# Seven block products in place of eight in the feed-forward networks, and one table function for the gate

## The chip, the cores and the metric

The kernel runs on one core of a Trainium2 chip. The metric is the time of one execution on the device in microseconds (us); the time before is the median of three runs, 1405.89 us (1405.14 to 1406.78). Engines: TensorE (PE) multiplies matrices, VectorE (DVE) and ScalarE (ACT) work element by element, GpSimd (POOL) does a few powers, and SyncE (SP) issues the weight loads. Matrix products end in PSUM, of which the kernel has six banks of 128 x 512 for products and two for transposes; all other tiles are in SBUF.

## The reference

256 rows of 1024 numbers go through two stacks. The first has one layer (attention, a chunked recurrent mixer, gates) and one feed-forward network. The second has two layers, each a feed-forward network, an attention stage with a memory, and a second feed-forward network. All five networks are of the same form, with 1024 inputs and 2816 hidden columns:

```python
def swiglu(h, w_gate, w_up, w_down):
    return (jax.nn.silu(h @ w_gate) * (h @ w_up)) @ w_down
...
        h = rmsnorm(x, ffn1_norm[i])
        x = x + 0.5 * swiglu(h, ffn1_w_gate[i], ffn1_w_up[i], ffn1_w_down[i])
```

All of it is float32. The networks take most of the span; the change is in them.

## The kernel before

**Splitting.** A float32 number is used as the sum of a rounded part (hi, type fp32r, tiles wh) and a rest (lo, tiles wl). `split` (L203) makes them: ACT casts (L204), DVE subtracts (L205). A product of two such numbers is three matmuls (`mm3`, L225): hi x hi, hi x lo, lo x hi. One matmul has 128 rows of output (a row tile t; there are two), 128 of contraction and 512 columns.

**The stream of weights.** The weights lie in DRAM as pieces of 128 x 2048 in the order of use. SP loads them into tiles `raw` (L199), three at a time and at most two pieces ahead. Each piece is split in two halves of 128 x 1024, each in two steps of 512 (`SPLIT_W`). A half is asked for by the matmuls (`half`, L220), and then halves up to four further are split (`SPLIT_AHEAD`). The results are in eight buffers (`W_BUFS`); a buffer is free when the matmuls on it have ended.

**A network** (`ffn_body`, L335) goes through its 2816 hidden columns in eleven blocks of 256 (j = 0 to 10). Gate-up (`gu`, L346): for each row tile a sum over 8 contraction steps into one PSUM bank, 256 gate columns beside 256 up columns, 24 matmuls on four halves. ACT takes the tanh of half the gate (th, L355), DVE makes silu from it (L356) and multiplies by the up part (hid, L358). `turn` (L369) transposes the hid of both row tiles on PE (4 transposes), and splits them into hh and hl (L381). Down (`dn`, L386): 12 matmuls for each row tile on two halves, summed over all blocks in two banks for each row tile; these four banks are taken for the whole network, so two are left for the gate-up products. The order is gu(0, j), dn(0, j-1), gu(1, j), dn(1, j-1) (L409): 72 matmuls and 4 transposes for a block.

**Order.** PE's order is written by hand; the class `Order` counts matmuls and puts transposes in where their data are due. On ACT, DVE and SP a scheduler sets the order when the program is built; what is marked `crit()` goes first. Once built, each engine works through its list in that order, and an instruction that waits holds all those behind it.

**Around the networks.** `boundary` (L309) transposes the new rows and makes the left operands uh and ul from uf (L299). The output projections of the attention stages go row tile by row tile (L1192), each over two column halves. `during` (L416) starts the preparation of the memory in the middle of a network.

## Time and profile before

| | |
|---|---|
| median of the runs | 1405.89 us |
| profiled execution | 1406.4 us, of which the span 1404.6 us |
| PE busy | 1385.3 us, 99% |
| DVE busy | 922.8 us, 66% |
| ACT busy | 763.6 us, 54% |
| one block of a network | 17.05 us |

The span goes from the first to the last instruction. A busy share is a mean over the span. A matmul's duration in the profile is longer than the distance to the next one, since matmuls overlap; the same is true, by less, of DVE and ACT. So what a row of many costs is read from start to start.

### The profile page before, as it was taken

The page shows a single profiled execution, that of the slowest core. Times are in us where ns is not written, and L with a number is a line of the kernel's source. Part 1 is how long each engine was busy: PE and PEld are TensorE (multiplying, and loading weights), DVE is VectorE, ACT ScalarE, POOL GpSimd, SP SyncE. Part 2 cuts the span into 40 slices and gives each one's busy share as a digit, 9 for nine tenths or more (in the row PEclk, how much of TensorE's full clock was granted, in tenths as well). Part 3 has the DMA queues.
Part 4 walks back from the last instruction along what each step waited for, and adds up shares of the span by engine and source line. Part 5 has one row for each costly group of instructions (what it writes and reads, how often), then busy time and mean ns, then how long its engine had stood idle before and what let it go on. Part 6 is the DMA issues. An engine that isn't in the chain of part 4 may idle for free.

```text
span 1404.6 us, 18011 instructions
## 1 busy us (share of the span) xinstructions
PE 1385.3 (99%) x6598; PEld 1126.6 (80%) x6598; DVE 922.8 (66%) x1789; ACT 763.6 (54%) x1527; POOL 58.2 (4%) x59
## 2 busy tenths in 40 slices
PE   8999999999999999999999999999999989999998
PEld 6777888888888888877888888888888767888887
DVE  7866587555585575768576665765756787755554
ACT  6556555444474454668565444644545568544442
POOL 0000000000010000022000000000000121000000
PEclk9999999999999999999999999999999999999999
DMA  8534546555446455454255555555454532455540
GB/s 291 174 122 158 180 142 237 192 191 189 180 157 233 180 180 180 168 197 161 91 183 191 195 187 194 207 191 197 164 206 155 182 120 94 172 188 194 192 180 30
DMA packets 37081, 246.59 MB, mean 176 GB/s; under 512 B 4736, under 2 KB 5760, under 8 KB 8064
## 3 DMA queue, kind: packets, MB, share of 16 engines
q1 hardware_dynamic: 35568, 243.09, 48.2%
q10 hardware_dynamic: 1424, 2.34, 0.5%
q8 instruction: 52, 0.85, 0.2%
q14 instruction: 37, 0.30, 0.1%
HBM read 244.37 MB, written 1.05 MB: 175 GB/s over the span
## 4 chain that ended last, share of the span: by engine, by line
PE 90%; DVE 6%; POOL 2%; ACT 1%; issue 1%; DMA 0%; SPq 0%; DVEq 0%; POOLq 0%; ACTq 0%
PE bank L149 86%; PE trbank L154 4%; POOL fac L261 2%; DVE wl L205 2%; DVE ms L953 1%; ACT p L454 1%; DVE nm L452 1%; DVE z L957 1%; DMA h<-in_x_dram 0%; DVE p L464 0%; DVE p L450 0%; DVE z L1015 0%; DVE p L1052 0%; DVE z L1017 0%; DVE z L1018 0%
## 5 line engine op out<-in xcount | busy, mean ns | idle before, releaser
L205 DVE TENSOR_TENSOR wl<-raw,wh 128x512 fp32r<-128x512 f32 x908 | 580.5, 686 | 194.4 <-ACT wh L204 187.6
L204 ACT CAST wh<-raw 128x512 fp32r<-128x512 f32 x908 | 513.0, 619 | 238.2 <-PE bank L149 227.9
L149 PE MATMUL bank<-wh,uh 128*128 128x512 f32 x1248 | 501.3, 402 | 0.0
L149 PE MATMUL bank<-wl,uh 128*128 128x512 f32 x1248 | 489.5, 392 | 0.0
L149 PE MATMUL bank<-wh,ul 128*128 128x512 f32 x1248 | 489.3, 392 | 0.0
L149 PEld LDWEIGHTS bank<-wh,ul 128*128 128x128 f32 x1248 | 234.6, 188 | 52.6
L149 PEld LDWEIGHTS bank<-wh,uh 128*128 128x128 f32 x1248 | 234.9, 188 | 48.8 <-issue 1.9
L149 PEld LDWEIGHTS bank<-wl,uh 128*128 128x128 f32 x1248 | 235.2, 188 | 46.1 <-DVE wl L205 0.3
L149 PE MATMUL bank<-wh,hh 128*128 128x512 f32 x440 | 172.8, 393 | 0.0
L149 PE MATMUL bank<-wl,hh 128*128 128x512 f32 x440 | 172.0, 391 | 0.0
L149 PE MATMUL bank<-wh,hl 128*128 128x512 f32 x440 | 172.0, 391 | 0.0
L355 ACT ACTIVATE th<-bank,rs 128x256 f32<-128x256 f32 x110 | 52.3, 475 | 179.2 <-PE bank L149 178.4
L356 DVE SCALAR_TENSOR_TENSOR th<-th,bank 128x256 f32<-128x256 f32 x110 | 46.3, 421 | 153.2 <-ACT th L355 153.2
L149 PEld LDWEIGHTS bank<-wl,hh 128*128 128x128 f32 x440 | 82.7, 188 | 18.0
L149 PEld LDWEIGHTS bank<-wh,hl 128*128 128x128 f32 x440 | 82.6, 188 | 17.9
L149 PEld LDWEIGHTS bank<-wh,hh 128*128 128x128 f32 x440 | 82.7, 188 | 17.6
L204 ACT CAST hh<-trbank 128x512 fp32r<-128x512 f32 (+1 forms) x60 | 33.1, 551 | 55.8 <-PE trbank L154 55.8
L261 POOL TENSOR_TENSOR r<-ms,mhalf 128x1 f32<-128x1 f32 x22 | 18.4, 838 | 909.5 <-DVE ms L271 909.5
L358 DVE SCALAR_TENSOR_TENSOR hid<-bank,rs,th 128x256 f32<-128x256 f32 x110 | 53.2, 484 | 3.6
L205 DVE TENSOR_TENSOR hl<-trbank,hh 128x512 fp32r<-128x512 f32 (+1 forms) x60 | 38.8, 646 | 16.5 <-ACT hh L204 13.5
L261 POOL TENSOR_TENSOR fac<-ms,mhalf 128x4 f32<-128x4 f32 (+2 forms) x26 | 38.4, 1477 | 246.8 <-DVE ms L954 139.3
L154 PEld LDWEIGHTS trbank<-cst,hid 128*128 128x128 f32 x220 | 27.6, 140 | 8.1
(223 smaller groups left out, 940.1 us busy)
## 6 DMA issues: line engine op xcount, KB each, us to landing
raw<-in_weights_dram SPq DMA_DIRECT2D x226, 1024.0 KB, 4.9
mem<-in_mem_dram ACTq DMA_DIRECT2D x4, 512.0 KB, 5.5
Tb<-in_rel_dram SPq DMA_DIRECT2D x3, 512.0 KB, 5.8
h<-in_x_dram SPq DMA_DIRECT2D x4, 256.0 KB, 3.8
raw<-in_weights_dram SPq DMA_DIRECT2D x2, 512.0 KB, 7.4
gf<-in_rows_dram SPq DMA_DIRECT2D x1, 512.0 KB, 4.1
out_dram<-h SPq DMA_DIRECT2D x2, 256.0 KB, 2.0
out_dram<-h SPq DMA_DIRECT2D x4, 128.0 KB, 1.8
```

The lines of the kernel that those rows point to most:

```text
L149: pe.matmul(out=out, lhsT=lhsT, rhs=rhs, start=start, stop=stop)
L154: pe.transpose(out=out, in_=in_, identity=ident if identity is None else identity)
L204: act.copy(out=hi, in_=src)
L205: dve.tensor_tensor(out=lo, in0=src, in1=hi.bitcast(F32), op=ALU.subtract)
L261: pool.tensor_tensor(out=dst, in0=src, in1=mhalf[:, 0:n], op=ALU.pow)
L355: act.activation(out=th, in_=acc[:, 0:256], func=AF.Tanh, scale=rh[t])
L356: dve.scalar_tensor_tensor(out=th, in0=th, scalar=1.0, in1=acc[:, 0:256], op0=ALU.add, op1=ALU.mult)
L358: dve.scalar_tensor_tensor(out=hd, in0=acc[:, 256:512], scalar=r2[t], in1=th, op0=ALU.mult, op1=ALU.mult)
L452: dve.tensor_reduce(out=nm, in_=s, axis=AX.X, op=ALU.max, negate=True)
L454: act.activation(out=p[:, j, a, 0:n], in_=s[:, j], func=AF.Exp, bias=nm[:, j:j + 1], accum_out=sums[:, j, a:a + 1])
L953: dve.tensor_reduce(out=ms, in_=sq, axis=AX.X, op=ALU.add)
L957: dve.tensor_tensor(out=v, in0=v, in1=fac.unsqueeze(2).to_broadcast([128, n, w]), op=ALU.mult)
```

## The change

The last six of the eleven blocks of each network are taken in three groups of two (`GROUPS`). For such a pair the gate-up product is a product of a 2 x 2 matrix of blocks (two row tiles by two halves of the contraction) with another (two halves of the contraction by two column blocks). It is computed as seven block products for eight, P1 to P7, each of 12 matmuls on two halves into one PSUM bank. Their right operands are sums of loaded pieces b11, b12, b21, b22, made by DVE in place (`add`: 8 of 128 x 1024 for a group) and then split like the others; three of the pieces are split as loaded. The left operands are four differences and sums of uf, made and split once in a network (`group_operands`, after block 0). The results are combined by DVE in tiles `jo` (`joined`, seven of 128 x 512 for a group; one more copy on ACT).

The order within a group on PE is P1, dn(1, a), dn(0, a), P6, P2, P5, dn(0, b), P7, dn(1, b), P3, P4, where a and b are two earlier blocks. Blocks 0 to 4 are computed as before, in the order gu(0, j), gu(1, j), dn(0, j-1), dn(1, j-1). The halves are now a list of jobs; the casts on ACT are held in the order of that list (`in_order`). A half is split in one step of 1024, and there are six operand buffers for eight. The pieces b12 and b22 get tiles of their own (`rawx`).

The gate is one ACT function, silu, with the row scale; the second DVE operation is gone. The output projections go column half by column half. The memory preparation starts after block 4 and has one tile for two.

```diff
 RAW_BUFS = 3
-W_BUFS = 8
+W_BUFS = 6
 C_BUFS = 11
 C2_BUFS = 10
 SPLIT_AHEAD = 4
 LOAD_AHEAD = 2
 CRIT = 300
-SPLIT_W = 512
+SPLIT_W = 1024
+
+GROUPS = 3
...
+    piece_at = {}
+
+    def add_job(key, piece, work):
+
+        at_job[key] = len(jobs)
+        jobs.append((key, piece, work))
+
+    def plain(i):
+        for m in range(2):
+            add_job((i, m), i, lambda i=i, m=m: raws[i][:, 1024 * m:1024 * m + 1024])
...
-            r = wp.tile([128, 2048], F32, tag="raw", bufs=RAW_BUFS, name="raw")
+            if i in kept:
+                r = kept[i][0].tile([128, 2048], F32, tag="tx", bufs=2, name="rawx")
+            else:
+                r = wp.tile([128, 2048], F32, tag="raw", bufs=RAW_BUFS, name="raw")
...
     def split(hi, lo, src):
-        act.copy(out=hi, in_=src)
+        c = act.copy(out=hi, in_=src)
         dve.tensor_tensor(out=lo, in0=src, in1=hi.bitcast(F32), op=ALU.subtract)
+        return c
+
+    order = [None]
+
+    def in_order(inst):
+
+        if order[0] is not None:
+            tc.add_manual_dep(inst.ins, order[0].ins.name,
+                              mybir.DependencyInfo(mybir.DependencyClass.NoSync, mybir.DependencyReason.DATA),
+                              reason="order of the operands")
+        order[0] = inst
...
+        while stream["split"] < min(n, len(jobs)):
+            key, piece, work = jobs[stream["split"]]
+            load_to(piece + 1 + LOAD_AHEAD)
+            r = work()
             hi = wp.tile([128, 1024], FR, tag="wh", bufs=W_BUFS, name="wh")
             lo = wp.tile([128, 1024], FR, tag="wl", bufs=W_BUFS, name="wl")
             for s in range(0, 1024, SPLIT_W):
-                split(hi[:, s:s + SPLIT_W], lo[:, s:s + SPLIT_W], r[:, 1024 * m + s:1024 * m + s + SPLIT_W])
-            parts[i, m] = (hi, lo)
+                in_order(split(hi[:, s:s + SPLIT_W], lo[:, s:s + SPLIT_W], r[:, s:s + SPLIT_W]))
+            parts[key] = (hi, lo)
             stream["split"] += 1
...
     def half(i, m, n):
-        split_to(2 * i + m + 1 + SPLIT_AHEAD)
+        split_to(at_job[i, m] + 1 + SPLIT_AHEAD)
...
+    def group_jobs(i, pool_, dn):
+
+
+        b11, b12, b22, b21 = i, i + 2, i + 3, i + 4
+        kept[b12] = kept[b22] = pool_
+        s = lambda m: slice(1024 * m, 1024 * m + 1024)
+        total = []
+
+        def job(name, piece, work):
+            for m in range(2):
+                add_job(((i, name), m), piece, lambda m=m: work(m))
+
+        def add(out, a, b):
+            dve.tensor_tensor(out=out, in0=a, in1=b, op=ALU.add)
+
+        def t2(m):
+            if m == 0:
+                total.append(pool_[0].tile([128, 2048], F32, tag="tn", bufs=1, name="tn"))
+            add(raws[b11][:, s(m)], raws[b11][:, s(m)], raws[b12][:, s(m)])
+            add(total[0][:, s(m)], raws[b11][:, s(m)], raws[b22][:, s(m)])
+            return total[0][:, s(m)]
+
+        def t3(m):
+            add(raws[b12][:, s(m)], raws[b12][:, s(m)], raws[b22][:, s(m)])
+            return raws[b12][:, s(m)]
+
+        def t4(m):
+            add(total[0][:, s(m)], total[0][:, s(m)], raws[b21][:, s(m)])
+            return total[0][:, s(m)]
+
+        job("P1", b11, lambda m: raws[b11][:, s(m)])
+        plain(dn[0])
+        job("P6", b22, t2)
+        job("P2", b21, lambda m: raws[b21][:, s(m)])
+        job("P5", b21, lambda m: raws[b11][:, s(m)])
+        plain(dn[1])
+        job("P7", b21, t3)
+        job("P3", b21, lambda m: raws[b22][:, s(m)])
+        job("P4", b21, t4)
...
+            s = tmp.tile([128, 4, 128], F32, tag="uf", bufs=4, name="uf") if keep is None else keep[:, k0:k0 + n]
+            full[id(u[2]), k0] = s
...
+        for g in range(GROUPS):
+            j = nc_ + 2 * g
+            a, b = (j - 2, j - 1) if g == 0 else (j - 1, j - 2)
+            plan["group", g] = i
+            plan["dn", a], plan["dn", b] = i + 1, i + 5
+            g0, g1 = source(("gu", j)), source(("gu", j + 1))
+            piece_at.update(enumerate((g0, source(("dn", a)), g1, g1 + 1, g0 + 1, source(("dn", b))), i))
+            group_jobs(i, plan["pool"], (i + 1, i + 5))
+            i += 6
+        for j in ((NJ - 2, NJ - 1) if GROUPS else ()):
+            take(("dn", j))
+            plain(plan["dn", j])
+        assert i == p0 + P_FFN
+        return plan
...
+        def element(t, j, acc):
+
+            hid_ready[t, j] = Ready()
             with crit():
                 th = fp.tile([128, 256], F32, tag="th", name="th")
-                act.activation(out=th, in_=acc[:, 0:256], func=AF.Tanh, scale=rh[t])
-                dve.scalar_tensor_tensor(out=th, in0=th, scalar=1.0, in1=acc[:, 0:256], op0=ALU.add, op1=ALU.mult)
-                hd = fp.tile([128, 256], F32, tag="hid", bufs=4, name="hid")
-                dve.scalar_tensor_tensor(out=hd, in0=acc[:, 256:512], scalar=r2[t], in1=th, op0=ALU.mult, op1=ALU.mult)
-            hids[t] = hd
-            hid_ready[t, j] = ev
-            if j == NJ - 1:
-                side.spawn(turn((t,), j))
-            elif t == 1:
-                side.spawn(turn((0, 1), j))
+                act.activation(out=th, in_=acc[:, 0:256], func=AF.Silu, scale=r[t])
+                hd = fp.tile([128, 256], F32, tag="hid", bufs=5, name="hid")
+                dve.scalar_tensor_tensor(out=hd, in0=acc[:, 256:512], scalar=r[t], in1=th, op0=ALU.mult, op1=ALU.mult)
+            hids[t, j] = hd
...
-        hids = [None, None]
-
-        def turn(ts, j):
-
-            mine = [hids[t] for t in ts]
-            yield 3.46
+        def turn(ts, j, wait):
+
+            yield wait
             n = len(ts)
-            hh = fp.tile([128, 4, 128], FR, tag=f"hh{n}{ts[0]}", name="hh")
-            hl = fp.tile([128, 4, 128], FR, tag=f"hl{n}{ts[0]}", name="hl")
+            hh = fp.tile([128, 2 * n, 128], FR, tag=f"hh{n}{ts[0]}", bufs=n, name="hh")
+            hl = fp.tile([128, 2 * n, 128], FR, tag=f"hl{n}{ts[0]}", bufs=n, name="hl")
...
-        def dn(t, j, kts=(0, 1)):
+        started = set()
+
+        def dn(t, j, kts=(0, 1), by_c=False):
...
+            done[t] += len(kts)
+            order = [(c, k) for c in range(2) for k in kts] if by_c else [(c, k) for k in kts for c in range(2)]
+            for n, (c, k) in enumerate(order):
+                wh, wl = half(plan["dn", j], k, 512)
+                first = (t, c) not in started
+                started.add((t, c))
+                mm3(accd[t][c], hh[:, k], hl[:, k], wh[:, c], wl[:, c], first,
+                    done[t] == 2 * NJ and (c, k) == [o for o in order if o[0] == c][-1])
+
+        done = [0, 0]
...
+        S = {}
+
+        def group_operands():
+            x11, x12, x21, x22 = (full.pop((id(u[t][2]), k)) for t in range(2) for k in (0, 4))
+            sh = fp.tile([128, 4, 4, 128], FR, tag="sh", bufs=1, name="sh")
+            sl = fp.tile([128, 4, 4, 128], FR, tag="sl", bufs=1, name="sl")
+
+            dve.tensor_tensor(out=x22, in0=x21, in1=x22, op=ALU.subtract)
+            dve.tensor_tensor(out=x21, in0=x11, in1=x21, op=ALU.subtract)
+            dve.tensor_tensor(out=x11, in0=x22, in1=x11, op=ALU.subtract)
+            dve.tensor_tensor(out=x12, in0=x12, in1=x11, op=ALU.add)
+            for n, (name, x) in enumerate((("P6", x11), ("P5", x22), ("P7", x21), ("P3", x12))):
+                split(sh[:, n], sl[:, n], x)
+                S[name] = sh[:, n], sl[:, n]
+            for name, t, k in (("P1", 0, 0), ("P2", 0, 4), ("P4", 1, 4)):
+                S[name] = u[t][0][:, k:k + 4], u[t][1][:, k:k + 4]
+
+        def group(g):
+
+            j = n_conv + 2 * g
+            a, b = (j - 2, j - 1) if g == 0 else (j - 1, j - 2)
+            last = g == GROUPS - 1
+            i = plan["group", g]
+
+            def joined(x, y, op, into=None):
+                o = fp.tile([128, 512], F32, tag="jo", bufs=4, name="jo") if into is None else into
+                with crit():
+                    dve.tensor_tensor(out=o, in0=x, in1=y, op=op)
+                return o
+
+            def prod(name):
+                acc = bank()
+                xh, xl = S[name]
+                for k in range(4):
+                    wh, wl = half((i, name), k // 2, 512)
+                    mm3(acc, xh[:, k], xl[:, k], wh[:, k % 2], wl[:, k % 2], k == 0, k == 3)
+                return acc
+
+            c11 = fp.tile([128, 512], F32, tag="jo", bufs=4, name="jo")
+            p1_ = prod("P1")
+            with crit():
+                act.copy(out=c11, in_=p1_)
+            dn(1, a)
+            dn(0, a)
+            U = joined(prod("P6"), c11, ALU.add)
+            joined(prod("P2"), c11, ALU.add, c11)
+            element(0, j, c11)
+            if last:
+                side.spawn(turn((0,), j, 4.2))
+            V = joined(prod("P5"), U, ALU.subtract)
+            dn(0, b)
+            p7 = prod("P7")
+            element(1, j + 1, joined(V, p7, ALU.subtract))
+            joined(p7, U, ALU.add, U)
+            if last:
+                side.spawn(turn((1,), j + 1, 4.9))
+            dn(1, b)
+            joined(prod("P3"), V, ALU.add, V)
+            element(0, j + 1, V)
+            side.spawn(turn((0,) if last else (0, 1), j + 1, 4.2))
+            joined(prod("P4"), U, ALU.add, U)
+            element(1, j, U)
+            side.spawn(turn((1,) if last else (0, 1), j, 4.2))
+
+        for j in range(n_conv):
+            more = 1 <= j < n_conv - 1
             gu(0, j)
-            if j:
+            gu(1, j)
+            if more:
                 dn(0, j - 1)
-            gu(1, j)
-            if j:
                 dn(1, j - 1)
-            if during and j == 5:
+            if j == 0:
+                group_operands()
+            if during and j == n_conv - 1:
                 during()
-        j = NJ - 1
-        gu(0, j)
-        dn(0, j - 1)
-        gu(1, j)
-        dn(1, j - 1, (0,))
+        for g in range(GROUPS):
+            group(g)
+        j = NJ - 2
         dn(0, j)
+        dn(1, j + 1, (0,))
+        dn(0, j + 1, by_c=True)
         fin(0)
-        dn(1, j - 1, (1,))
-        dn(1, j)
+        dn(1, j + 1, (1,))
+        dn(1, j, by_c=True)
         fin(1)
...
             u2, r2 = [], []
-            for t in range(2):
-                for c in range(2):
+            for c in range(2):
+                for t in range(2):
                     acc = lin(mT[t], (p2 + 2 * c, p2 + 2 * c + 1))
                     sl = h[t][:, 512 * c:512 * c + 512]
                     with crit():
                         dve.scalar_tensor_tensor(out=sl, in0=acc, scalar=0.5, in1=sl, op0=ALU.mult, op1=ALU.add)
-                u2.append(boundary(t, h[t], gcol(G_FFN1B)))
-                r2.append(row_rstd(h[t]))
+                    if c:
+                        u2.append(boundary(t, h[t], gcol(G_FFN1B)))
+                        r2.append(row_rstd(h[t]))
...
-            ms = mp.tile([128, 1024], F32, tag="mem", bufs=2, name="mem")
+            ms = mp.tile([128, 1024], F32, tag="mem", bufs=1, name="mem")
```

DVE's order in the first network, before: block 1's gate and block 2's. wl is the rest of a weight half, hl that of a transposed hid.

```order
L356 SCALAR_TENSOR_TENSOR th<-th,bank 128x256
L358 SCALAR_TENSOR_TENSOR hid<-bank,rs,th 128x256
L205 TENSOR_TENSOR wl<-raw,wh 128x512 x6
L356 SCALAR_TENSOR_TENSOR th<-th,bank 128x256
L358 SCALAR_TENSOR_TENSOR hid<-bank,rs,th 128x256
L205 TENSOR_TENSOR wl<-raw,wh 128x512 x6
L205 TENSOR_TENSOR hl<-trbank,hh 128x512
```

Now, from the join of P4 of the first group to the split of the sum for P6 (tn) of the second group and of P2:

```order
L551 TENSOR_TENSOR jo<-bank,jo 128x512
L267 TENSOR_TENSOR raw<-raw,rawx 128x1024
L464 SCALAR_TENSOR_TENSOR hid<-jo,r,th 128x256
L267 TENSOR_TENSOR tn<-raw,rawx 128x1024
L223 TENSOR_TENSOR hl<-trbank,hh 128x512 x2
L223 TENSOR_TENSOR wl<-tn,wh 128x1024
L267 TENSOR_TENSOR raw<-raw,rawx 128x1024
L267 TENSOR_TENSOR rawx<-rawx 128x1024
L267 TENSOR_TENSOR tn<-raw,rawx 128x1024
L267 TENSOR_TENSOR rawx<-rawx 128x1024
L267 TENSOR_TENSOR tn<-tn,raw 128x1024
L223 TENSOR_TENSOR wl<-tn,wh 128x1024
```

Between the last hid of a pair and the second half of P6's operand there stand the two hl, seven of the eight adds and two splits, where a block had its splits of 512 between two gates.

The middle of the second group on DVE, from the join of P7 (into two tiles) to the join of P4:

```order
L551 TENSOR_TENSOR jo<-jo,bank 128x512
L551 TENSOR_TENSOR jo<-bank,jo 128x512
L464 SCALAR_TENSOR_TENSOR hid<-jo,r,th 128x256
L223 TENSOR_TENSOR wl<-tn,wh 128x1024
L267 TENSOR_TENSOR tn<-tn,raw 128x1024
L551 TENSOR_TENSOR jo<-bank,jo 128x512
L223 TENSOR_TENSOR wl<-tn,wh 128x1024
L464 SCALAR_TENSOR_TENSOR hid<-jo,r,th 128x256
L223 TENSOR_TENSOR wl<-raw,wh 128x1024
L551 TENSOR_TENSOR jo<-bank,jo 128x512
```

The joins, which need a product that PE has ended, stand between splits and adds that need none of it; the join of P3 stands ahead of the split of P4's second half.

## Rows read from the trace of the kernel before

**Rows 1.** The page's head, busy shares, and TensorE's granted clock in 40 slices

```profile
span 1404.6 us, 18011 instructions
PE 1385.3 (99%) x6598; PEld 1126.6 (80%) x6598; DVE 922.8 (66%) x1789; ACT 763.6 (54%) x1527; POOL 58.2 (4%) x59
...
PEclk9999999999999999999999999999999999999999
```

**Rows 2.** Who PE waited for: us in total, times, longest

```profile
PE trbank L154 <- DMA cst<-in_consts_dram: 4.0, 1, 4.0
PE trbank L154 <- DVE z L1018: 3.3, 2, 2.3
PE trbank L154 <- DVE p L1052: 2.2, 1, 2.2
...
PE bank L149 <- ACT qkT L1026: 0.7, 1, 0.7
```

**Rows 3.** Timeline of PE inside a network: start, us, instruction

```profile
339.68 0.39 PE L149 MATMUL bank<-wh,ul 128*128 128x512 f32 x1
...
345.23 0.40 PE L149 MATMUL bank<-wh,ul 128*128 128x512 f32 x1
345.46 0.60 PE L154 MATMUL trbank<-cst,hid 128*128 128x128 f32 x4
345.82 0.48 PE L149 MATMUL bank<-wh,uh 128*128 128x512 f32 x1
```

**Rows 4.** Timeline of DVE over the same block

```profile
334.15 0.48 DVE L358 SCALAR_TENSOR_TENSOR hid<-bank,rs,th 128x256 f32<-128x256 f32 x1
...
342.45 0.48 DVE L358 SCALAR_TENSOR_TENSOR hid<-bank,rs,th 128x256 f32<-128x256 f32 x1
342.85 3.69 DVE L205 TENSOR_TENSOR wl<-raw,wh 128x512 fp32r<-128x512 f32 x6
...
351.20 0.48 DVE L358 SCALAR_TENSOR_TENSOR hid<-bank,rs,th 128x256 f32<-128x256 f32 x1
```

**Rows 5.** That block as a window: PE, PEld, DVE, ACT, POOL busy, clock, DMA

```profile
334.15:351.20 17.05, 17.05 (x78) 13.91 (x76) 9.93 (x18) 8.23 (x15) 0.00 (x0) 1.00 0.51 186
```

**Rows 6.** Groups of DVE instructions by form: count, busy us, mean ns, idle before

```profile
L205 DVE TENSOR_TENSOR wl<-raw,wh 128x512 fp32r<-128x512 f32 x908 | 580.5, 686 | 194.4 <-ACT wh L204 187.6
L358 DVE SCALAR_TENSOR_TENSOR hid<-bank,rs,th 128x256 f32<-128x256 f32 x110 | 53.2, 484 | 3.6
L356 DVE SCALAR_TENSOR_TENSOR th<-th,bank 128x256 f32<-128x256 f32 x110 | 46.3, 421 | 153.2 <-ACT th L355 153.2
...
L1269 DVE TENSOR_TENSOR h<-h,gf 128x1024 f32<-128x1024 f32 x2 | 2.4, 1219 | 0.0
```

**Rows 7.** Timeline of DVE at the first network's end

```profile
399.81 1.22 DVE L1269 TENSOR_TENSOR h<-h,gf 128x1024 f32<-128x1024 f32 x1
400.94 0.69 DVE L205 TENSOR_TENSOR ul<-uf,uh 128x512 fp32r<-128x512 f32 x1
```

**Rows 8.** Groups of ACT instructions by form

```profile
L204 ACT CAST wh<-raw 128x512 fp32r<-128x512 f32 x908 | 513.0, 619 | 238.2 <-PE bank L149 227.9 <-DMA raw<-in_weights_dram 5.2 <-ACT wh L204 2.8
L355 ACT ACTIVATE th<-bank,rs 128x256 f32<-128x256 f32 x110 | 52.3, 475 | 179.2 <-PE bank L149 178.4 <-DVE hl L205 0.7
...
L267 ACT ACTIVATE junk<-h 128x1024 f32<-128x1024 f32 x18 | 19.0, 1058 | 24.7 <-DVE h L1197 19.8 <-DMA h<-in_x_dram 2.9 <-DVE h L402 1.5
...
L182 ACT ACT_TABLE_LOAD x1 | 1.3, 1283 | 1.7 <-PEq L1406 1.7
```

**Rows 9.** Waits between ACT, DVE and PE around the splits

```profile
ACT wh L204 <- PE bank L149: 227.9, 231, 5.2
DVE wl L205 <- ACT wh L204: 187.6, 72, 5.0
```

**Rows 10.** Weight loads: size and median time to landing

```profile
raw<-in_weights_dram SPq DMA_DIRECT2D x226, 1024.0 KB, 4.9
```

**Rows 11.** Windows by microsecond behind a gap on PE, and PE's timeline there

```profile
1128.00:1129.00 1.00, 0.00 (x0) 0.00 (x0) 1.00 (x4) 1.00 (x3) 0.00 (x0) 0.94 0.00 0
1129.00:1130.00 1.00, 0.50 (x3) 0.52 (x4) 1.00 (x4) 0.41 (x1) 0.00 (x0) 0.50 0.00 0
...
1132.00:1133.00 1.00, 1.00 (x7) 0.81 (x6) 1.00 (x3) 1.00 (x6) 0.00 (x0) 0.86 0.80 197
1129.50 0.66 PE L154 MATMUL trbank<-cst,p 128*128 128x128 f32 x2 [2.18 <-DVE p L1052]
...
1130.38 0.63 PE L149 MATMUL bank<-wl,uh 128*128 128x512 f32 x1
1130.81 0.63 PE L149 MATMUL bank<-wh,ul 128*128 128x512 f32 x1
```

More of the change, by code (lines that the diff above doesn't have):

```diff
@@ L198, in load_to @@
                 w = 2048 // n_dma
-                nc.sync.dma_start(out=r[:, w * q:w * q + w], in_=weights[i, :, w * q:w * q + w])
+                nc.sync.dma_start(out=r[:, w * q:w * q + w], in_=weights[piece_at.get(i, i), :, w * q:w * q + w])
             raws[i] = r
@@ L287, in new_u @@
         return uh, ul, []
+    full = {}
     def put_T(u, k0, n, src, gains=None, gain1=None, keep=None):
@@ L297, in put_T @@
         if gains is not None:
-            s = tmp.tile([128, 4, 128], F32, tag="uf", name="uf") if keep is None else keep[:, k0:k0 + n]
+            s = tmp.tile([128, 4, 128], F32, tag="uf", bufs=4, name="uf") if keep is None else keep[:, k0:k0 + n]
+            full[id(u[2]), k0] = s
             dve.tensor_tensor(out=s, in0=b3, op=ALU.mult,
@@ L333, in ffn, with ffn_plan, source, take @@
             ffn_body(fp, *args)
+    def ffn_plan(p0):
+        plan = {"pool": [None]}
+        i = p0
+        def source(key):
+            kind, j = key
+            if kind == "dn":
+                return p0 + (3 * j + 4 if j < NJ - 1 else 32)
+            return p0 if j == 0 else p0 + 3 * j - 1
+        nc_ = NJ - 2 * GROUPS
+        def take(key, n=1):
+            nonlocal i
+            plan[key] = i
+            for q in range(n):
+                piece_at[i + q] = source(key) + q
+            i += n
+        for j in range(nc_):
+            take(("gu", j), 2)
+            if 1 <= j < nc_ - 1:
+                take(("dn", j - 1))
+        for j in range(nc_):
+            for q in range(2):
+                plain(plan["gu", j] + q)
+            if 1 <= j < nc_ - 1:
+                plain(plan["dn", j - 1])
+        for g in range(GROUPS):
[12 more added lines that the diff above has]
+        return plan
@@ L335, in ffn_body @@
     def ffn_body(fp, p0, u, r, res_scale, finish, during=None):
[L336 removed]
+        plan = plans[p0]
+        plan["pool"][0] = fp
         accd = [None, None]
[L338 to L351 removed]
+        hidT, hid_ready, hids = {}, {}, {}
@@ L376, in turn @@
             b = trbank()
-            for a, hd in enumerate(mine):
+            for a, t in enumerate(ts):
+                hd = hids.pop((t, j))
                 for i in range(2):
@@ L390, in dn @@
             hh, hl = hidT[t, j]
-            order = [(c, k) for c in range(2) for k in kts] if j == NJ - 1 else [(c, k) for k in kts for c in range(2)]
-            for c, k in order:
-                wh, wl = half(dnp(j), k, 512)
-                mm3(accd[t][c], hh[:, k], hl[:, k], wh[:, c], wl[:, c], j == 0 and k == 0, j == NJ - 1 and k == 1)
+            done[t] += len(kts)
[7 more added lines that the diff above has]
+        done = [0, 0]
         def fin(t):
@@ L407, in fin @@
                 finish(t)
-        for j in range(NJ - 1):
+        S = {}
[12 more added lines that the diff above has]
+                S[name] = u[t][0][:, k:k + 4], u[t][1][:, k:k + 4]
@@ L1191, in second_mix @@
         res = [[], []]
-        for t in range(2):
-            for c in range(2):
+        for c in range(2):
+            for t in range(2):
                 acc = lin((get_oT(t)[0], get_oT(t)[1], o_ready[t]), (p1 + 2 * c, p1 + 2 * c + 1))
@@ L1245, in memory_kv, with plan_ffn @@
             side.spawn(task())
-    P_FFN = 3 * NJ
+    plans = {}
+    for n in range(30):
+        plain(n)
+    p = 30
+    def plan_ffn():
+        nonlocal p
+        plans[p] = ffn_plan(p)
+        p += P_FFN
+    plan_ffn()
+    for layer in range(2):
+        plan_ffn()
+        for n in range(16):
+            plain(p + n)
+        p += 16
+        plan_ffn()
+    assert p == NP
     p = 0
```

32 lines of the change are left out of this document (13 added, 19 removed).

## The prediction

> **What bounds the kernel now.** I read the page's shares first, then the waits of PE, then one steady stretch of a feed-forward network engine by engine. PE is busy for 99% of the span at a granted clock of full speed, DVE for 66%, ACT for 54% [rows 1]. The waits confirm that PE is the bound and not only busy: its longest waits are the first load (4.0 us) and a few single ones in the attention stages, some 16 us in all, none of them in a feed-forward network [rows 2]. A network is a chain of matmuls that never stops. Their starts go from 339.68 to 345.23 us in 24 steps, 0.2313 us each; four transposes take another 0.36 us [rows 3]. One block (72 matmuls, 4 transposes) repeats every 17.05 us (hid at 334.15 and at 351.20) [rows 4], and in that window DVE is busy for 9.93 us, ACT for 8.23 [rows 5]. So a matmul that goes saves time only as long as DVE and ACT keep up with the operands of those that stay. That is the question here.
>
> **What PE loses.** A pair of blocks costs 2 x 2 x 24 = 96 matmuls in the gate-up products; as a group it costs 7 x 12 = 84. Three groups in five networks: 180 fewer, 180 x 0.2313 = 41.6 us. That is all the change can give.
>
> **What DVE gains, and where.** Durations: 512-wide operations follow each other at 0.600 us ((3.69 - 0.69)/5, the six splits at 342.85) and a hid is 0.40 us before its successor (342.45 to 342.85) [rows 4]. A 1024-wide tensor_tensor stands in this trace too: 1.219 us long [rows 6], its successor starts 1.13 us after it (399.81 to 400.94) [rows 7]; I use 1.133 (0.600 plus 512 x the 0.533/512 by which 1.219 exceeds 0.686). Adds and splits are the same operation on the same sizes and get the same price.
>
> Per group DVE has 18 splits (14 for the seven products, 4 for the two down blocks), 8 adds, all 1024 wide: 26 x 1.133 = 29.5 us. To that 7 joins (512) 4.2, 4 hid 1.6, 2 hl 1.2: 36.5 us. The gate's second DVE operation (th, 0.42 us) [rows 6] is gone and already left out. PE needs 132 x 0.2313 + 0.7 = 31.2 us for a group, and the same two blocks took 34.1 us before. DVE is thus slower than PE in a group by 5.3 us and slower than the old PE time by 2.4. Over a whole network the mean hides this: 84 splits, 24 adds, 21 joins, 8 operand steps, 22 hid and 11 hl make some 155 us against 756 x 0.2313 + 4 = 179 for PE. But a split is made at most four halves ahead and there are six buffers, so DVE's free time in the first five blocks can't be spent on the groups, but for what stands early in its order.
>
> How much stands early I count in the order. Let T0 be PE's end of the gate-up product of block 4, tile 1 (then P1 starts). The hid of that product ends at T0 + 1.1 (its activation 0.48, itself 0.48, hand-overs). By then 6 adds of group one and the splits of P1 and of the first down block are done: ten operations, 11.3 us of credit. Behind it, up to the last split of P4 in group three, DVE has 68 operations of 1024, 25 of 512 and 11 of 256: 77.0 + 15.0 + 4.4 = 96.4 us. After that split PE still has 6 matmuls of P4, 48 of the last two down blocks and transposes: 13.3 us. So the network can't end before T0 + 1.1 + 96.4 + 13.3 = T0 + 110.8, whatever PE does. Before, the same work was 480 matmuls, 480/72 x 17.05 = 113.7 us; PE alone would now need 105.3. Without one wait on DVE the gain is 2.9 us a network, 14.5 in five, instead of 41.6.
>
> **What DVE waits for.** Walking DVE's order against PE's with these durations, it does wait. Group one: it has the split of P3 done at T0 + 19.8, but the next, P4's first half, takes the buffers of P7's first half, which PE leaves at T0 + 21.6, and ACT's cast (about 1.0 us: 512 take 0.62, a 1024-wide ACTIVATE 1.06) [rows 8] comes between: 2.9 us. Some 1 us more where down-block buffers come free late. At each group's end the two hl wait for transposes and casts behind P1: 0.4 each. Group two: the join of P2 0.5, a hid behind its activation 0.4, the join of P3 1.7 (after P7 PE has 24 matmuls, 5.6 us; DVE has two joins, hid, a split and an add, 3.9). Group three much the same. I take 8 us a network, 40 in five. Below it is bounded by 0; above by 1.7 at four joins in each group, 20 us a network. Today's DVE waits in a split are mostly for ACT (187.6 us in 72 waits), ACT's for PE to leave a buffer (227.9 in 231) [rows 9]: the same two hand-overs, now with DVE behind them.
>
> **The rest.** Two networks have the memory preparation moved from block 5 to block 4's end, inside group one: 8 operations of 512, 4.8 us each time; half falls into the 2.9 us wait, so 5 us in all (0 to 9.6). The operands of the products (4 subtractions, 4 splits of 512, 4.8 us) lie beside blocks 0 and 1, where PE has 11.1 us for every four halves and DVE 4.5 + 0.8 of its own: nothing; without that cover 24 us. Table loads on ACT go from 3 to 8, 1.28 us each [rows 8]; the first gate of a network waits, but its PSUM bank is wanted 11 us later: nothing. Splits of 1024 for 512 take 30 us off DVE in all, nothing where PE is the bound. Six operand buffers for eight leave two halves ahead instead of four in the projections, and the output projections now go column by column: the first tile's transposes have 24 matmuls (5.6 us) of cover for a chain of about 3.6. I put both at 0, between -3 and +10. The weight loads stay 1 MB and 4.9 us [rows 10]; the buffers that they wait for are freed over 10 us before the data is wanted: nothing.
>
> [...] In my walk PE stands for 2.4 us within P6 of group two and for 2.2 us ahead of P6 of group three. [...]
>
> **The sum**, against the profiled execution's 1406.4 us (span 1404.6 and 1.8 around it): 1406.4 - 14.5 + 40 + 5 + 6 = 1442.9. The median of the runs is 0.5 below the profiled one: 1442.
>
> **Rivals.**
> *DVE saturated but never waiting.* If the order happens to fit, the waits are gone: 1406.4 - 14.5 + 9.6 = 1401. For it: ACT has some 22 us a group (18 casts of 1.0, four gates of 0.48, a copy and two casts of 0.6), so its casts can run ahead. Against it: at every join DVE stands in order behind a product that PE has not ended.
> *PE stays the bound*, the side on which the change pays: 1406.4 - 41.6 = 1365. It decides at 31.2 us of DVE a group; it would need 1024-wide operations at 0.93 us, faster than the 1.13 of [rows 7], or a credit of 17 us where the order shows 11.3. I see nothing for it but the mean share.
> [...]
>
> **Chances.** Forecast 0.67, with a range of its own of 1415 to 1466; saturated without waits 0.14 (1396 to 1408); PE bound 0.06; starved 0.13. The range of 8 in 10 reaches from 1402 to 1474: outside lie PE bound, half of the saturated case and two thirds of the starved one. About 0.2% (2.8 us) is what a measurement can tell from no change. Faster: PE bound and a little under half of the saturated case, 0.12; the same: the other half, 0.07; slower 0.81.
>
> **What would show it.** In the three groups of a network DVE should be busy 90% or more and a group should last 36 to 40 us, with PE waiting for wl, longest at P6 of groups two and three; blocks 0 to 4 should keep 17.05 us. The join operations should be 0.69 us long, adds and splits 1.22. Granted clock below full speed should stand only behind PE's gaps. If the groups take 31 us and PE shows no wait for DVE, the step that counts DVE's 96.4 us is wrong; if DVE is below 80% busy there while PE waits too, the waits are mis-sized.

## The result and the profile after

The changed kernel takes **1458.1 us** (median of four runs, 1456.0 to 1459.9) against 1405.8: a ratio of 1.037, 95% interval 1.0353 to 1.0389. It is slower by 52.4 us; 1442 was predicted, with 1402 to 1474 around it. The profiled execution took 1458.2 us.

The page of the changed kernel, to be held against [rows 1]:

```profile
span 1456.4 us, 17114 instructions
PE 1383.2 (95%) x6418; PEld 1093.6 (75%) x6418; DVE 1165.1 (80%) x1565; ACT 831.6 (57%) x1208; POOL 57.4 (4%) x59
...
PE   8999999999899989999999998999899989999998
...
DVE  8856577799985999967575999868999777767997
```

PE has the 180 matmuls less, and its digits now fall to 8 in the networks, where DVE's rise to 9. The waits of PE say for whom (us in total, times, longest); none of these six is in [rows 2]:

```profile
PE bank L152 <- DVE wl L223: 29.3, 41, 1.8
PE bank L152 <- ACT hh L222: 6.4, 15, 0.9
PE trbank L157 <- DVE rs L638: 4.2, 2, 3.2
...
PE bank L152 <- DVE hl L223: 3.7, 5, 1.4
PE bank L152 <- ACT wh L222: 3.2, 7, 0.7
...
PE bank L152 <- ACT uh L222: 2.0, 1, 2.0
```

DVE's operations have the durations that the forecast named (count, busy us, mean ns), 1.22 us for a split or an addition of 1024 [rows 6] and 0.69 for a join:

```profile
L223 DVE TENSOR_TENSOR wl<-raw,wh 128x1024 fp32r<-128x1024 f32 x424 | 512.3, 1221 | 114.9 <-ACT wh L222 107.0
...
L551 DVE TENSOR_TENSOR jo<-bank,jo 128x512 f32<-128x512 f32 x90 | 61.9, 688 | 17.6 <-PE bank L152 17.5
...
L267 DVE TENSOR_TENSOR tn<-raw,rawx 128x1024 f32<-128x1024 f32 x30 | 36.1, 1219 | 0.0
```

Two windows of the first network, each from the first hid of a group to that of the next (columns as in [rows 5]): 33.2 and 37.1 us, with DVE busy for 94 and 96% of it. (The first hid of a group comes at no fixed place in PE's work: the windows hold 125 and 136 matmuls, where a group has 132.) PE is idle for 2.2 and 2.8 us of them, and the matmuls behind their waits at P6 take longer themselves (0.49 us at 332.60 and 0.50 at 367.83, the row below, for 0.39 to 0.40 of those around them).

```profile
305.40:338.60 33.20, 30.97 (x135) 24.07 (x133) 31.05 (x35) 20.48 (x25) 0.00 (x0) 1.00 0.31 109
338.60:375.70 37.10, 34.33 (x144) 25.87 (x145) 35.66 (x40) 19.99 (x24) 0.00 (x0) 1.00 0.48 173
```

The longest wait in the second is the one of the forecast, at P6. DVE's timeline ahead of it, and the row of PE (last):

```profile
359.68 1.29 DVE L223 TENSOR_TENSOR hl<-trbank,hh 128x512 fp32r<-128x512 f32 x2
360.88 2.35 DVE L267 TENSOR_TENSOR raw<-raw,rawx 128x1024 f32<-128x1024 f32 x2
363.15 2.35 DVE L267 TENSOR_TENSOR tn<-raw,rawx 128x1024 f32<-128x1024 f32 x2
365.42 1.22 DVE L267 TENSOR_TENSOR rawx<-rawx 128x1024 f32<-128x1024 f32 x1
366.56 2.35 DVE L223 TENSOR_TENSOR wl<-tn,wh 128x1024 fp32r<-128x1024 f32 x2
```
```profile
367.83 0.50 PE L152 MATMUL bank<-wl,sh 128*128 128x512 f32 x1 [1.79 <-DVE wl L223]
```

Five additions stand in a row without a gap, one of them (rawx, at 365.42) for P7, which comes much later, and only then the split that PE wants. DVE doesn't wait there; it has too much to do, and part of it stands ahead of its time. Ahead of the second half of P6 in the second group, where PE waits 1.57 us (332.60), six additions stand behind the last hid, not seven as the section on the change says, and three of the six are for P7 and P4. No run moves them back in DVE's order, so what that order alone costs is open.

**Where the 52 us are.** The first and the last hid of each network, read from DVE's timeline, cut the span into stages. The table sums them, in us, with 12 matmuls (2.8 us a network) put back into the networks, since the new order leaves 48 matmuls behind the last hid for 36:

| | before | no groups (e1) | after |
|---|---|---|---|
| five networks, first to last hid | 860.3 | 860.3 | 894.0 |
| network to network (two) | 33.5 | 34.6 | 41.8 |
| the two attention stages | 277.9 | 288.4 | 288.2 |
| start and end | 232.9 | 232.0 | 232.4 |

So 34 us come in the networks, 8 from network to network, and 10 in the attention stages, which have no group at all. Of the 8, some 4.6 are network 4's own: PE goes from its last matmul of network 3 (929.17) to the first of network 4 (929.40) without a stop, but ACT stands for the memory's load ahead of the first gate, and so the first hid comes late:

```profile
939.94 1.06 ACT L336 ACTIVATE junk<-mem 128x1024 f32<-128x1024 f32 x1 [5.40 <-DMA mem<-in_mem_dram]
...
941.00 0.46 ACT L462 ACTIVATE th<-bank,r 128x256 f32<-128x256 f32 x1
```

Read on PE instead, to the last matmul of a network, from its first hid (networks 1, 3, 5) or its first matmul (2 and 4), the five networks cost 5.3, 12.3, 6.4, 10.9 and 4.4 us more than before, 39.3 in all. Another 2.2 lie ahead of network 2 and 10.3 in the attention stages: together the 51.8 us between the two spans.

### The profile page after: what moved, and what is told of

It is laid out like the page before. It is cut to its first block, busy times and chain, and to the rows that moved or that the text cites. A ratio compares the mean times of both kernels' runs of the same rounds, so it can differ in the third digit from the quotient of the medians.

```text
span 1456.4 us, 17114 instructions
## 1 busy us (share of the span) xinstructions
PE 1383.2 (95%) x6418; PEld 1093.6 (75%) x6418; DVE 1165.1 (80%) x1565; ACT 831.6 (57%) x1208; POOL 57.4 (4%) x59
## 4 chain that ended last, share of the span: by engine, by line
PE 66%; DVE 25%; issue 3%; ACT 2%; DMA 2%; POOL 1%; SPq 0%; DVEq 0%; POOLq 0%; ACTq 0%
PE bank L152 63%; DVE wl L223 11%; PE trbank L157 3%; DVE jo L551 3%; DVE tn L267 2%; DVE rawx L267 1%; DVE raw L267 1%; POOL fac L330 1%; DVE hid L464 1%; DVE hl L223 1%; ACT wh L222 1%; DVE nm L633 1%; DMA mem<-in_mem_dram 1%; DMA Tb<-in_rel_dram 0%; DVE ms L1135 0%
## 5 line engine op out<-in xcount | busy, mean ns | idle before, releaser
L223 DVE TENSOR_TENSOR wl<-raw,wh 128x1024 fp32r<-128x1024 f32 x424 | 512.3, 1221 | 114.9 <-ACT wh L222 107.0
L222 ACT CAST wh<-raw 128x1024 fp32r<-128x1024 f32 x424 | 436.1, 1048 | 157.6 <-PE bank L152 149.9
L152 PE MATMUL bank<-wh,uh 128*128 128x512 f32 x948 | 381.2, 402 | 2.0 <-ACT uh L222 2.0
L152 PE MATMUL bank<-wl,uh 128*128 128x512 f32 x948 | 375.6, 396 | 3.0 <-DVE wl L223 2.2
L152 PE MATMUL bank<-wh,ul 128*128 128x512 f32 x948 | 374.4, 395 | 0.2 <-DVE ul L223 0.2
L152 PE MATMUL bank<-wl,sh 128*128 128x512 f32 x240 | 98.3, 409 | 24.0 <-DVE wl L223 24.0
L152 PEld LDWEIGHTS bank<-wh,hh 128*128 128x128 f32 x440 | 82.7, 188 | 26.6 <-ACT hh L222 10.9
L152 PE MATMUL bank<-wh,sh 128*128 128x512 f32 x240 | 97.5, 406 | 3.2 <-ACT wh L222 3.2
L152 PE MATMUL bank<-wh,sl 128*128 128x512 f32 x240 | 96.3, 401 | 0.0
L223 DVE TENSOR_TENSOR wl<-tn,wh 128x1024 fp32r<-128x1024 f32 x60 | 72.3, 1219 | 5.3 <-ACT wh L222 5.3
L551 DVE TENSOR_TENSOR jo<-bank,jo 128x512 f32<-128x512 f32 x90 | 61.9, 688 | 17.6 <-PE bank L152 17.5
L223 DVE TENSOR_TENSOR wl<-rawx,wh 128x1024 fp32r<-128x1024 f32 x60 | 70.6, 1219 | 0.0
```

The source lines that it names most:

```text
L152: pe.matmul(out=out, lhsT=lhsT, rhs=rhs, start=start, stop=stop)
L222: c = act.copy(out=hi, in_=src)
L223: dve.tensor_tensor(out=lo, in0=src, in1=hi.bitcast(F32), op=ALU.subtract)
L551: dve.tensor_tensor(out=o, in0=x, in1=y, op=op)
```

## The experiments

Each kernel is the changed one but for what its diff shows, or the kernel named. Each is timed beside the kernel before, which took 1405.3 to 1406.1 us.

**e1: no group.** Eleven plain blocks; the last two are taken in the order of the kernel before.

```diff
-GROUPS = 3
+GROUPS = 0
```


> No group at all (eleven plain blocks in each network); all other edits stay: silu as one function, halves split in one step of 1024, six operand buffers, both gate-up products ahead of both down products, output projections column by column. Theory A (the 52 us come from DVE's work in and right behind three consecutive groups): 1406, between 1400 and 1412. Rival B (the other edits and the stages between the networks carry much of it: fewer buffers, table loads, other order of projections): 1420 to 1445.

1418.4 us, ratio 1.009 (1.0078 to 1.0108). Neither was quite right: 39.7 us come with the groups, but 13.1 with the other edits (each against the kernel before of its own round). The networks are untouched (table above); the attention stages lose 10.5. Of these 4.6 are longer waits of PE, most of the growth for ACT's copies (qkT and oh, 3.6 us for 0.7), and 3.4 two more drops of the granted clock; the rest is open. The first place of loss, ACT and PE of this kernel:

```profile
625.93 1.98 ACT L222 CAST wh<-raw 128x1024 fp32r<-128x1024 f32 x2
628.75 0.59 ACT L657 COPY pt<-trbank 128x512 f32<-128x512 f32 x1 [0.84 <-PE trbank L157]
629.23 0.48 ACT L1206 ACTIVATE qkT<-trbank,gqk 128x256 f32<-128x256 f32 x1
629.60 0.37 ACT L1207 COPY qkT<-trbank 128x256 f32<-128x256 f32 x1
```
```profile
630.03 1.78 PE L152 MATMUL bank<-qkT 64*128 64x256 f32 x8 [1.31 <-ACT qkT L1207]
```

and the same place before:

```profile
624.75 0.46 ACT L1025 ACTIVATE qkT<-trbank,gqk 128x256 f32<-128x256 f32 x1
625.10 0.36 ACT L1026 COPY qkT<-trbank 128x256 f32<-128x256 f32 x1
625.36 2.18 ACT L204 CAST wh<-raw 128x512 fp32r<-128x512 f32 x4
```

The short qkT copies stand behind two casts and the copy pt (transposed attention weights) now, where they stood ahead of both; pt itself stands 0.84 us for PE's transposes. PE waits 1.31 us for qkT, and the granted clock falls behind it (0.59 and 0.55 in the two windows of 2 us from 630). The last thing ahead of qkT is pt, so it is the order of ACT's list, set when the program is built, that costs here, and not the length of the casts alone. In e9 below (three halves ahead) pt is behind qkT again at this place, and PE's wait for it is gone:

```profile
641.60 1.03 ACT L222 CAST wh<-raw 128x1024 fp32r<-128x1024 f32 x1
642.54 0.46 ACT L1207 ACTIVATE qkT<-trbank,gqk 128x256 f32<-128x256 f32 x1
642.91 0.35 ACT L1208 COPY qkT<-trbank 128x256 f32<-128x256 f32 x1
644.40 0.59 ACT L658 COPY pt<-trbank 128x512 f32<-128x512 f32 x1 [1.14 <-PE trbank L157]
```

**e2: one group, e10: two groups.** `GROUPS = 1` and `GROUPS = 2`. The memory preparation starts right ahead of the first group here too, that is after block 8 and after block 6.

> One group in each network in place of three, in blocks 9 and 10. Theory A: DVE comes into a group with 11.3 us of work done ahead, and a single group asks it for 5.3 us more than PE has, so PE stays nearly the bound: 60 matmuls x 0.2313 = 13.9 us less than without groups, minus a few us for the late end: 1392 to 1403. Rival B (each group costs by itself, by waits at its joins and buffers): a third of the excess, 1418 to 1428. Rival C (a fixed cost of each network's end): 1435 or more.

> Two groups in each network, one behind the other, in the changed kernel's order. One group took 1418.0, none 1418.4, three 1458.1. Theory (the first group lives on the lead that the plain blocks left, each group behind it pays in full: 37 us for the 34.1 of two plain blocks, and a late end): 1432 to 1442, so the second group costs about as much as the third. Rival (the cost comes with the third alone, at the network's end): 1418 to 1425.

1418.0 (ratio 1.009, 1.0075 to 1.0105) and 1433.9 (1.0203, 1.0188 to 1.0219). With none and three: 1418.4, 1418.0, 1433.9, 1458.1. The first group costs nothing, the second 16 us (1433.9 lies in the range of its theory), the third 24: each group behind the first adds, as DVE's lead is used up. That the first would gain (1392 to 1403) was wrong. Read on PE as above, networks 1, 3 and 5 do gain 1.5, 1.8 and 2.3 us of the 2.8 that 12 matmuls less are worth; networks 2 and 4, where the preparation runs into the group, lose 0.6 and 1.5, and 2.2 are lost ahead of network 2.

**e3: no additions.** The products P6, P5, P7 and P4 take pieces as loaded, so the sums are left out of the computation; matmuls, splits and joins stay.

```diff
...
-            add(raws[b12][:, s(m)], raws[b12][:, s(m)], raws[b22][:, s(m)])
             return raws[b12][:, s(m)]
...
-            add(total[0][:, s(m)], total[0][:, s(m)], raws[b21][:, s(m)])
-            return total[0][:, s(m)]
+            return raws[b21][:, s(m)]
```


> Three groups, but the eight additions of operand pieces in each group are left out: the loaded pieces b22, b12 and b21 are split in place of the sums (this part of the computation is left out; matmuls, splits, joins and loads are as in the changed kernel). DVE then has 27.4 us a group, PE 31.2. Theory A (DVE's sum of work): PE is the bound again, 1365 to 1385. Rival (the waits of DVE for PE's products and for buffers, not its work): 1400 to 1420. Rival (stages between the networks): 1440 or more.

1397.5 us (0.9948, 0.9933 to 0.9963). 60.7 us less than the changed kernel, and PE's waits for wl fall from 29.3 us to 0.4: DVE's work is what PE waited for.

```profile
PE bank L152 <- DVE wl L223: 0.4, 1, 0.4
```

But it lies between the two ranges, 21 us below e1 and not 41.6. Three groups in a row also wait where DVE has time: PE stood 4.5 us for hl, 3.7 for hh and 3.3 for hid. These 11.5, and 2.0 ahead of network 2 with 1.7 of low clock behind it, are 15 of the missing 21; the rest is open.

**e4: the additions on GpSimd.**

```diff
-            dve.tensor_tensor(out=out, in0=a, in1=b, op=ALU.add)
+            pool.tensor_tensor(out=out, in0=a, in1=b, op=ALU.add)
```


> Three groups, the eight additions of a group on GpSimd instead of VectorE. No trace of this case shows GpSimd on 128x1024. If an addition takes it up to 2.5 us (20 us a group) and leaves DVE alone: 1370 to 1395, faster than both kernels. If it takes over 4 us (32 us a group, more than PE's 31.2), or holds DVE's operations back while it runs: 1440 to 1500.

1605.3 us (1.1432, 1.1413 to 1.1451), the second of the two expectations, and worse. An addition takes 2.4 to 3.4 us on GpSimd, and DVE is held up beside it. Both engines' rows:

```profile
289.25 3.24 POOL L267 TENSOR_TENSOR tn<-raw,rawx 128x1024 f32<-128x1024 f32 x1
292.45 3.38 POOL L267 TENSOR_TENSOR rawx<-rawx 128x1024 f32<-128x1024 f32 x1
295.79 6.76 POOL L267 TENSOR_TENSOR tn<-tn,raw 128x1024 f32<-128x1024 f32 x2
```
```profile
293.90 3.01 DVE L223 TENSOR_TENSOR wl<-tn,wh 128x1024 fp32r<-128x1024 f32 x1
296.83 6.80 DVE L223 TENSOR_TENSOR wl<-raw,wh 128x1024 fp32r<-128x1024 f32 x2
303.55 0.68 DVE L223 TENSOR_TENSOR hl<-trbank,hh 128x512 fp32r<-128x512 f32 x1
304.15 3.48 DVE L223 TENSOR_TENSOR wl<-raw,wh 128x1024 fp32r<-128x1024 f32 x3
```

Two splits take 6.80 us while GpSimd adds; once it is done (302.55), three take 3.48. What PE then waits for is not the splits (2.1 us) but the hid behind them in DVE's order: 119.3 us in 26 waits.

**e5, e6, e12: the 13 us without groups.** e5 is e1 with `W_BUFS = 8`; e12 is e5 with `SPLIT_W = 512` as well; e6 is the kernel before with silu alone.

```diff
...
-                act.activation(out=th, in_=acc[:, 0:256], func=AF.Tanh, scale=rh[t])
-                dve.scalar_tensor_tensor(out=th, in0=th, scalar=1.0, in1=acc[:, 0:256], op0=ALU.add, op1=ALU.mult)
+                act.activation(out=th, in_=acc[:, 0:256], func=AF.Silu, scale=r[t])
...
```


> As the kernel without groups, but with eight operand buffers for six. That kernel took 1418.4 for 1405.3. Theory (six buffers: ACT's cast stands for a buffer and holds the casts and copies behind it, that PE then waits for): 1405 to 1409. Rival (halves split in one step of 1024, and the table loads of silu: their length in ACT's list delays the short operations whatever the buffers): 1413 to 1419.

> The kernel before with one part of the change alone: the gate as one silu function (one DVE operation less for each gate, table loads on ACT between silu and the exponentials). DVE is not the bound there; if the table loads are hidden: 1403 to 1407. If the one of them that stands ahead of the exponentials of the attention stages is what the kernel without groups lost: 1410 to 1418.

> As the kernel without groups and with eight buffers (1414.2), but a half is split in two steps of 512 again, as before. What is left of the change is silu (1.8 us alone), the order gate-up, gate-up, down, down, the output projections by column half, and the earlier memory preparation. If the casts of 1024 delay the short operations behind them in the attention stages: 1405 to 1409. If the order of the projections does: 1411 to 1415.

1414.2 (1.0062, 1.0047 to 1.0077), 1407.5 (1.0017, 1.0007 to 1.0027) and 1409.0 (1.0029, 1.0019 to 1.0038). For e5 it was the rival that held, e6 lies 0.5 us above its first range, e12 in its first. So of the 13.1: two buffers less 4.2, splits of 1024 for 512 5.2, silu 1.8, and 1 to 2 that stay with the orders and the one memory tile, each known to some 2 us. By one trace of each, they don't sit in the same place. The attention stages lose 3.9 us with silu alone, 2.0 more with the orders, 0.6 with splits of 1024 and 4.0 with six buffers; the 5.2 of the splits lie in the start (2.6) and from network to network (1.7), where no row here shows their cause.

**e7: the groups spread; e8: with three halves ahead; e11: with the memory preparation last.** The three groups stand between plain blocks, and a network ends with a plain block. e8 adds `SPLIT_AHEAD = 3`; e11 is e8 with the memory preparation (`during()`) begun ahead of block 10 instead of behind block 4.

```diff
-GROUPS = 3
+SEQ = (("P", 0, ()), ("P", 1, ()), ("G", 2, (0, 1)), ("P", 4, (3,)), ("G", 5, (2, 4)), ("P", 7, (6,)),
+       ("G", 8, (5, 7)), ("P", 10, (9, 8, 10)))
...
-        for g in range(GROUPS):
-            group(g)
+        for kind, j, downs in SEQ[:-1]:
+            if kind == "G":
+                group(j, *downs)
+                continue
...
```


> The same three groups, spread over the network: blocks 0 and 1, group 2-3, block 4, group 5-6, block 7, group 8-9, block 10; the memory preparation ahead of block 4. Work of every engine as in the changed kernel, only the order differs, and a network ends with a plain block as before. Theory (DVE's free time lies in the plain blocks and can't be carried over more than four halves): between groups DVE comes to its full lead again, a group costs about what PE asks, 1418 - 41.6 = 1377, with up to 1 us of waits in each group: 1377 to 1395. Rival (each group costs by its own waits, wherever it stands): 1440 to 1458.

> The spread order, with a half split at most three halves ahead instead of four. With six buffers the fourth half ahead often stands on ACT for a buffer that PE still reads, and holds other ACT work back. If that head-of-line wait is what costs at the networks' ends and in the attention stages, this is 5 to 12 us below the spread order with four. If DVE's lead into a group matters more, it is 5 to 15 us above it.

> The spread order with three halves ahead, and the memory preparation of two networks moved from block 4 to ahead of block 10, behind which no group comes. In the spread order these two networks take 163.0 and 160.6 us from first to last gate product, the others 154 to 156, and PE waits for DVE in them alone. If the preparation's DVE operations beside a group are the cause: 8 to 12 us less, 1368 to 1373. If it is the preparation's own place on PE and ACT, wherever it stands: 1377 to 1382.

1384.4 (0.9848, 0.9834 to 0.9863), 1380.1 (0.9819, 0.9804 to 0.9833) and **1377.3** (0.9799, 0.9785 to 0.9814): all three faster than both kernels. In e7 PE's waits for wl are down to this:

```profile
PE bank L153 <- DVE wl L224: 5.9, 7, 1.7
```

The third network from first to last hid, before, after and in e8 (each from its own trace):

```profile
718.79:890.06 171.27, 171.27 (x773) 140.89 (x772) 101.69 (x176) 83.87 (x156) 0.00 (x0) 1.00 0.51 185
```
```profile
743.52:918.38 174.86, 167.56 (x727) 132.69 (x726) 147.72 (x160) 98.21 (x119) 0.00 (x0) 0.99 0.48 165
```
```profile
711.43:865.68 154.25, 154.25 (x699) 127.20 (x698) 146.70 (x160) 98.10 (x117) 0.00 (x0) 1.00 0.53 188
```

DVE is busy for 147.7 and 146.7 us, the same work; but PE doesn't stand for a moment in the last. (36 matmuls more than before, 8.3 us, lie behind the last hid there; 171.3 - 8.3 for these and 8.3 saved is 154.7.) From network to network e8 takes 24.7 and 23.6 us, that is 16.4 and 15.3 without those 8.3, for 17.5 and 16.0 before: with a plain block last the networks' ends cost nothing. e8 gave 4.3 us, just short of the 5 to 12 expected. e11 gave 2.7 and ends at the edge of its second range, so the preparation's place beside a group is not the main cause. The two networks with memory preparation went from 163.0 and 160.6 to 160.8 and 158.4; what still makes them 4 to 6 us longer than the others (0.2 and 2.3 before) is open.

**e9: the changed kernel with three halves ahead.** `SPLIT_AHEAD = 3`, its order kept.

> The changed kernel with its order, a half split at most three halves ahead instead of four. If ACT's casts that stand for one of the six buffers and hold the short casts behind them (hh in the groups, uh at the networks' ends) are a cost of their own, as the 4 us that this gave in the spread order suggest: 1440 to 1455. If DVE's lead of four halves into the first group is worth more: 1460 to 1475.

1453.3 us (1.0343, 1.0326 to 1.036), in the first range. But PE's waits for wl (29.6 us) and hh (6.3) are as in the changed kernel, so the reason given is not shown in the groups, and the 1.99 us ahead of network 2 stay too. Half of the gain is in the attention stages (140.4 and 149.9 us for 142.8 and 151.0), the rest in the start and from network to network; in the first attention stage the order of ACT's list, shown with e1, is the visible part.

## Why the prediction was right, and where its sizes were off

**PE is bound by DVE in the groups: shown.** e3 takes DVE's additions away and PE's waits for wl go; e7 keeps all the work and gives DVE its time between the groups, and they shrink to 5.9 us. The rival in which DVE is full but nothing waits (1401) and the one in which PE stays the bound (1365) are out; the second is what the spread order comes near to. PE didn't starve either: the waits that the rows show in the networks are some 42 us, near the forecast's 40. Of the signs named, DVE's share (94 and 96%), the durations and the plain blocks (17.02 us for 17.05, from hid to hid) came. From the first down product of a group to that of the next, in the first network, the first group lasted 32.4 us, where 36 to 40 were named for all, and the second 36.6.

**The chain from T0 held.** The forecast ended a network at T0 + 110.8 and some 8 us of waits: 118.8. In the first network the hid is at 288.74, so T0 is 287.6, and the last matmul starts at 407.39 and its successor could start 0.23 later: T0 + 120.0. Networks 3 and 5 end at T0 + 120.6 and 117.6. The waits in these stretches sum to 7.3, 9.7, 7.9, 9.8 and 7.5 us, 42 for the 40 predicted, and the places were right: the second half of P6 in group two and its first half in group three hold 17.7 of the 29.3 us for wl, each 1.6 to 1.8 us, where 2.4 and 2.2 were said. By PE's rows the networks cost 39.3 us more, where 36.5 were predicted (-14.5 + 40 + 5 + 6).

**The memory preparation** was put at 5 us in groups. Networks 2 and 4 end at T0 + 126.2 and 124.7. Without the drops of the clock (below: 3.4 and 1.7 us there, 0 and 1.7 in networks 1 and 3) they take 3.4 us more than networks 1 and 3; in e1, where the preparation starts at the same block, it was 1.4. So some 2 us in each, 4 in all, near the 5. From hid to hid all of it would seem to lie in network 2, since network 4's first hid is late.

**Failed: the other edits at 0.** Projections, buffers, 1024-wide splits and table loads were put at nothing (the first two "at 0, between -3 and +10"), because PE's cover was taken to be enough: 24 matmuls, 5.6 us, for a chain of about 3.6. e1 measured 13.1. In an attention stage PE waits for single short operations of ACT and DVE (in e1 2.8 us in two waits for qkT, 3.2 in one for rs), and at the place shown with e1 the order of ACT's list decides, not ACT's share. This is the larger part of the 16 us by which the forecast was low: of the profiled 15.3, the attention stages have 10.3, the gap ahead of network 2 has 2.2, the networks 2.8.

**Failed: "Six operand buffers for eight ... I put both at 0", at the networks' ends too.** ACT and PE at the end of the first network after:

```profile
403.70 1.05 ACT L222 CAST wh<-raw 128x1024 fp32r<-128x1024 f32 x1
407.12 1.05 ACT L222 CAST wh<-raw 128x1024 fp32r<-128x1024 f32 x1 [2.37 <-PE bank L152]
408.08 1.05 ACT L336 ACTIVATE junk<-h 128x1024 f32<-128x1024 f32 x1
...
409.12 0.60 ACT L222 CAST uh<-uf 128x512 fp32r<-128x512 f32 x1
```
```profile
409.78 0.50 PE L152 MATMUL bank<-wh,uh 128*128 128x512 f32 x1 [1.99 <-ACT uh L222]
```
```profile
410.00:412.00 2.00, 2.00 (x7) 1.28 (x7) 1.64 (x3) 2.00 (x3) 1.41 (x1) 0.79 1.02 430
412.00:414.00 2.00, 2.00 (x9) 1.60 (x8) 0.82 (x3) 1.27 (x3) 0.60 (x2) 0.50 1.01 418
```

The cast uh, which the next network's first matmul needs, stands behind a cast for the stream that waits 2.37 us until PE leaves a buffer, and behind junk (the sum of squares of a row). PE then waits 1.99 and runs for some 3 us at half the clock (0.79 and 0.50 in these windows, 0.86 in the next: 1.7 us lost). The same wait is in the kernel with one group (403.21 us, 1.99) and in e3, so it doesn't take a late DVE; with a plain block last (e7, e8) it is gone. It comes once, ahead of network 2; ahead of network 4 PE doesn't stand. That six buffers make it is read from these rows and not shown: no run has groups with eight.

**The clock.** In windows of 2 us, 13.6 us of PE's time are lost to a low clock after and 5.1 in e1: 8.5 with the groups. No run shows the 6 us that stand for it in the forecast's sum; in their place the traces show five drops of 1.7 us, as much as the one in the trace of before, where the clock was 0.94, 0.50, 0.50, 0.50 and 0.86 in the five windows of [rows 11], of which these are the third and the fourth:

```profile
1130.00:1131.00 1.00, 1.00 (x4) 0.81 (x4) 1.00 (x3) 0.69 (x2) 0.00 (x0) 0.50 0.00 0
1131.00:1132.00 1.00, 1.00 (x4) 0.80 (x3) 1.00 (x3) 0.75 (x4) 0.00 (x0) 0.50 0.24 33
```

One of the five is behind the 1.99 us ahead of network 2, and four are inside networks, each behind a wait of 1.8 us at P6 (534.05, 570.65, 888.35, 1088.88). A wait of that size is not always followed by a fall: of the ten waits of 1.6 to 1.8 us at P6 four were, and in the two groups shown above the granted clock stayed at 1.00. What sets the four apart no run shows, so that 8.5 came out near 6 is in part luck.

**How much the hit says.** The range of 8 in 10 was 72 us wide. Inside it the waits and their places were right by the rows, but 12.5 us came from stages that were put at nothing (attention 10.3, ahead of network 2 2.2).

## What to carry to other kernels

A mean share hides where an engine is full (here 80% for DVE in the mean, 94 and 96% in two groups): count its work for each stretch that can't borrow from the next, here as far as the lead of four halves reaches, and mix heavy and light stretches before the work itself is made smaller. When an in-order engine gets longer operations or fewer buffers, look at the short operations behind them that the bound engine waits for, in the stages where its share is low too. Of the 41.6 us that the matmuls left out are worth on PE, the spread order got 34 (e7 against e1) where the first order lost 40: the order of the same work decided between +52 us and -21 against the kernel before, and three halves ahead with the preparation last made it -29.

## What was not expected of the hardware

In e4 VectorE's operations with both operands in SBUF took longer beside an addition on GpSimd: a split 3.4 us for 1.2, and a hid made from SBUF 2.60 for 0.48, while a join with one operand in PSUM kept its 0.68. In the mean of the whole run a hid made from SBUF took 0.98 us, one made from PSUM 0.48. The addition at 339.18, most of it while DVE stood for ACT, took 2.35, those beside splits 2.5 (at 330.12) to 3.4:

```profile
327.84 2.60 DVE L464 SCALAR_TENSOR_TENSOR hid<-jo,r,th 128x256 f32<-128x256 f32 x1
330.37 3.37 DVE L223 TENSOR_TENSOR wl<-raw,wh 128x1024 fp32r<-128x1024 f32 x1
333.66 0.68 DVE L551 TENSOR_TENSOR jo<-bank,jo 128x512 f32<-128x512 f32 x1
```
```profile
332.62 3.32 POOL L267 TENSOR_TENSOR rawx<-rawx 128x1024 f32<-128x1024 f32 x1
...
339.18 2.35 POOL L267 TENSOR_TENSOR rawx<-rawx 128x1024 f32<-128x1024 f32 x1
```

That GpSimd loses as well rests on the one addition at 339.18; what lengthens DVE's operations beside it no trace here shows.
